# First layer's MLP: the last six pairs of hidden blocks by seven products, gated sums added to x by accumulating DMAs, squares on ScalarE

## The chip, the cores and the metric

One core of one Trainium2 chip runs the whole program. The metric is the device time of one execution in microseconds: 1545.13, 1548.43 and 1548.74 in three runs, median 1548.43. The profile's names for the engines are PE (TensorE's matmuls), PEld (its weight loads), DVE (VectorE), ACT (ScalarE), POOL (GpSimd) and SP (SyncE, which issues most of the DMAs).

## The reference

An inference step of a transformer with two layers over 640 tokens (512 latent, 128 context) of width 1024, with different weights in each layer. Each layer has a mixer and then an MLP with 4096 hidden columns; both read a normalised x that is shifted and scaled, and both add their output to x times a gate. Shift, scale and gate (six vectors of 1024 per layer, one set for latent and one for context tokens) come from a conditioning vector by a matrix product, the adaLN modulation. Cut to what matters:

```python
def squared_relu_mlp(h, w1, w2):
    return jnp.square(jax.nn.relu(h @ w1)) @ w2

def modulate(x, g, shift, scale):
    return rmsnorm(x, g) * (1 + scale) + shift

def trunk_layer(x, mod, p, mix_fn):
    shift1, scale1, gate1, shift2, scale2, gate2 = jnp.split(mod, N_MOD, axis=-1)
    y, ctx_state = mix_fn(modulate(x, p['norm1'], shift1, scale1))
    x = x + gate1 * y
    x = x + gate2 * squared_relu_mlp(modulate(x, p['norm2'], shift2, scale2), p['w1'], p['w2'])
    return x, ctx_state
```

## The kernel before

**Layout.** Features lie on the 128 partitions, tokens along the free dimension; x is one SBUF tile of 8 blocks of 128 features by 640 tokens. A product over all tokens is made in two halves of 384 and 256 tokens (HALVES). The context tokens have gates of their own, so the gated sum of a second half is two instructions of 128 columns (REGIONS).

**Precision.** Every operand is split in two fp32r parts, a rounded one and the remainder, and every product is three matmuls (mm3, lines 248 to 250). A weight unit of 128x1024 is loaded by SP into one of three raw buffers; ScalarE casts it (line 239), VectorE makes the difference (line 240); the result takes one of four `hl` buffers.

**The MLP.** The 4096 hidden columns go in eight groups of 512. A group has two pairs of hidden blocks, each pair 2 x 128 columns. The first product gives a pair's hidden values, which are squared after the relu and split; the second product multiplies a group's four hidden tiles with its rows of the second weight and adds the gated result to x, for eight blocks of output features (m) and two token halves. In program order the first product of group j+1 stands before the second product of group j.

A plain pair makes 96 matmuls of 384 or 256 columns, 320 on average; a group's second product makes 192. After a plain product ScalarE does the relu (line 1139) and the rounded square (line 1140), the full square is made by POOL in the first layer (line 1144) and by ScalarE in the second (line 1142), and VectorE takes the difference (line 1145).

**Seven products.** In the second layer, pairs 2 to 15 are made another way: each pair's product is seen as 2x2 blocks (two halves of the features by two hidden blocks; 320 tokens each) and made by seven products instead of eight, 84 matmuls of 320 columns. For this Blocks.sums makes sums and differences of blocks of the normalised activations once per layer, strip by strip (four strips), from an unsplit copy `hf` that ScalarE keeps (Blocks.keep); Pair.w2 makes four sums of weight blocks per pair (lines 1162 to 1172). Pair.rest puts the results together on VectorE and squares them at the end (Pair.square, lines 1195 to 1197). The first layer does all sixteen pairs plainly.

**Gated sums.** gate_add (line 428) reads the PSUM bank, multiplies by the gate and adds to x, on VectorE: one instruction for a first half, two for a second one.

**adaLN tiles.** ada_steps and ada_tile (lines 168 to 179) make 128 modulation values for both sets of tokens: a 512 KB load into one of the same three raw buffers and two instructions on VectorE (line 174). 80 of these stand in the first layer: 24 before its MLP, 56 in it. The first eight of the 56 give gate2, the gate of this very MLP; the other 48 are the second layer's. They stand in the program between the weight units of both products: eight in a group, twelve in the first.

**What sets the order.** The kernel writes its operations in program order; a planner of the framework, which has a time model of its own, orders each engine's list from it, with the program order as priority. Buffers come from pools: `a` (12 of 2x640), `b` (6 of the same), `p` (5 of 640: relu and square tiles `rr` and `rq`), `t2` (3 of 384), raw (3) and hl (4); PSUM has four single banks and two double ones.

Of the kernel before, what the change touches and what calls it, by code (L numbers as in the profile page):

```python
# [56 lines left out]
def step_kernel(ctx, tc, xT, wf, wt, wt3, wo1, wo2, wq, wkvs, wada, wnat, wnat2, vec, rows, fnorm, cvec, cache, kpec,  # L57
# [29 lines left out]
    def nm(s):  # L87
        uid[0] += 1
        return f"{s}_{uid[0]}"
# [30 lines left out]
    def f(ap):  # L120
        return ap.bitcast(F32)
# [269 lines left out]
    class Blocks(Modulate):  # L391
# [8 lines left out]
        def sums(self, s):  # L400
            if s == 0:
                self.op = {k: [None] * 4 for k in ("b11", "b21", "b22", "t1", "t2", "t3", "t4")}
            op = self.op
            if s % 2 == 0:
                t3 = phase["me"].tile([128, 2, 2, HT], F32R, tag="t3", bufs=1, name=nm("t3")) if s else \
                    tb([128, 2, 2, HT], "t3")
                for k, two in (("t2", ta([128, 2, 2, HT], "t2")), ("t3", t3), ("t1", ta([128, 2, 2, HT], "t1"))):
                    op[k][s], op[k][s + 1] = two[:, 0], two[:, 1]
            h1, h2 = self.h[s], self.h[4 + s]
            op["b11"][s], op["b21"][s], op["b22"][s] = h1[:, :, :HT], h2[:, :, :HT], h2[:, :, HT:]  # L410
            op["t4"][s] = h1[:, :, HT:]
            fx = self.hf[s]
            b11, b12, b21, b22 = fx[:, 0, :HT], fx[:, 0, HT:], fx[:, 1, :HT], fx[:, 1, HT:]
            t3, t2_ = tmp2([128, HT], "t3"), tmp2([128, HT], "t2")
            nc.vector.tensor_sub(t3, b12, b22)
            nc.vector.tensor_sub(b12, b11, b12)
            nc.vector.tensor_add(t2_, b22, b12)
            nc.vector.tensor_sub(b21, b21, t2_)
            for k, src in (("t2", t2_), ("t3", t3), ("t1", b12), ("t4", b21)):
                split(op[k][s][:, 0, :], op[k][s][:, 1, :], src)  # L420
# [15 lines left out]
    def layer(l, h, next_norm, nxt):  # L436
# [669 lines left out]
        mod.step(0, K_PAIRS[6])  # L1106
        mod.step(0, K_PAIRS[7])
        close_phase()
        if blocks:
            open_phase(f"mlp{l}", me=1)  # L1110

        me = phase.get("me")

        class Pair:

# [3 lines left out]

            def __init__(self, p, u=None):
                self.p = p
                pool = (lambda: me.tile([128, 2, TOK], F32R, tag="u", bufs=2, name=nm("u"))) if p % 3 == 0 \
                    else (lambda: tb([128, 2, TOK], "u"))
                self.u = u or [pool(), pool()]
                self.r, self.q = [None] * 2, [None] * 2

            def plain(self, us, i, half, tail=None):

                t0, n = HALVES[half]
                ps = bank("w1")
                u, ui = us[i], self.u[i]
                for z, k in enumerate(K_PAIRS):
                    mm3(ps[:, :n], (u[:, 0, 128 * k:128 * (k + 1)], u[:, 1, 128 * k:128 * (k + 1)]),
                        act(mod.h, k, t0, n), z == 0, z == KT - 1)
                r, q = tp([128, 384], "rr")[:, :n], tp([128, 384], "rq")[:, :n]
                hh = ui[:, 0, t0:t0 + n]
                nc.scalar.activation(r, ps[:, :n], AF.Relu)  # L1139
                nc.scalar.activation(hh, r, AF.Square)  # L1140
                if blocks:
                    nc.scalar.activation(q, r, AF.Square)
                else:
                    nc.gpsimd.tensor_mul(q, r, r)  # L1144
                nc.vector.tensor_sub(ui[:, 1, t0:t0 + n], q, f(hh))

            def load(self):
# [81 lines left out]
            return x_.u  # L1229

        def two_plain(j):
            get = ta if j % 2 == 0 else tb
            two = [Pair(2 * j + i, [get([128, 2, TOK], "u") for _ in range(2)]) for i in range(2)]
            for i in range(4):
                w = load_unit(wf[l, U_W1 + 4 * j + i])
                for half in range(2):
                    two[i // 2].plain([w, w], i % 2, half)
                if l == 0:
                    ada_steps(2 if j == 1 else 1)
            return two[0].u + two[1].u  # L1240

        def mlp2_tile(ut, u, m, half, nrm):
# [5 lines left out]
            gate_add(ps, m, half, l, 40, nrm)  # L1248

        def mlp2(j, ut):  # L1250
            if j < 7:
                for i in range(4):
                    u = load_unit(wf[l, U_W2 + 4 * j + i])
                    for m in (2 * i, 2 * i + 1):
                        for half in range(2):
                            mlp2_tile(ut, u, m, half, None)
                    if l == 0:
                        ada_steps(1)
            else:
                us = [load_unit(wf[l, U_W2 + 4 * j + i]) for i in range(4)]  # L1260
                for m in range(8):
                    mlp2_tile(ut, us[m // 2], m, 0, next_norm)
                for m in range(8):
                    mlp2_tile(ut, us[m // 2], m, 1, next_norm)
                    if m >= 2:
                        nxt.step(0, m - 2)
                for half, k in ((0, 6), (0, 7)) + tuple((1, k) for k in range(KT)):
                    nxt.step(half, k)

        head = [Pair(p, None if blocks else [ta([128, 2, TOK], "u") for _ in range(2)]) for p in range(2)]  # L1270
# [8 lines left out]
        if blocks:  # L1279
            for s in range(4):  # L1280
                mod.sums(s)
            mlp2(0, us)
            us = full(2) + full(3)
            for j in range(1, 8):
                if j < 7:
                    nxt_us = full(2 * j + 2)
                mlp2(j, us)
                if j < 7:
                    us = nxt_us + full(2 * j + 3)
            close_phase()  # L1290
            del phase["me"]
        else:
            for j in range(8):
                cur = us
                if j < 7:
                    us = two_plain(j + 1)
                mlp2(j, cur)


    open_phase("mix0", lay=1, pt=3)  # L1300
# [152 lines left out]
```

## Time and profile before

| | us |
|---|---|
| median of three runs | 1548.43 |
| profiled execution | 1544.02 |
| its span | 1542.1 |
| PE busy | 1473.7 (96%) |
| DVE busy | 1131.9 (73%) |
| ACT busy | 668.9 (43%) |
| POOL busy | 248.2 (16%) |
| the first layer's MLP | 342.6 to 805.5 |
| the second layer's MLP | 1089.8 to 1533 |

Times inside the span are counted from its start. Busy time is what an engine spent in instructions that the profile counts as work; register, semaphore and DMA-issuing instructions are not in it. PE's matmuls are pipelined, so a busy PE is not PE at its peak. The granted clock is the share of full speed that TensorE was allowed: 1.00 is 2.4 GHz. In a row of the timeline, the bracket says how long the engine had stood before the instruction and what released it.

### The profile page before, as it was taken

How to read it: one execution, taken by the hardware profiler on the slowest of the kernel's cores; microseconds unless marked ns; L12 is line 12 of the kernel's file. 1: busy time of each engine (PE TensorE's matmuls, PEld its weight loads, DVE VectorE, ACT ScalarE, POOL GpSimd, SP SyncE). 2: the span in 40 equal slices, each digit the busy share in tenths (PEclk: the TensorE clock that was granted, in tenths of full speed). 3: DMA queues.
4: the chain of work that ended last, by engine and by line, in shares of the span. 5: the costliest groups of instructions: out<-in, count | busy, mean ns of one | idle time of the engine just before them, and what ended most of it. 6: DMA issues, size and time to landing. Idle time of an engine off the chain costs nothing.

```text
span 1542.1 us, 25203 instructions
## 1 busy us (share of the span) xinstructions
PE 1473.7 (96%) x9716; PEld 1415.8 (92%) x9716; DVE 1131.9 (73%) x2210; ACT 668.9 (43%) x1400; POOL 248.2 (16%) x245
## 2 busy tenths in 40 slices
PE   6898999989999999999999999998999999999997
PEld 2698988979999999999999989898899999999996
DVE  5988878869978778876458666686886676566655
ACT  3544556745222322232236445675835244324422
POOL 2133103343211210120021110222300000000002
PEclk9899999999999999999999989999999999999999
DMA  8544321333555455444212311011222223123211
GB/s 312 199 136 139 100 66 45 103 94 111 190 164 164 139 151 162 151 142 146 66 48 64 123 43 37 30 49 45 83 69 96 69 83 96 57 81 96 83 55 69
DMA packets 50103, 160.22 MB, mean 104 GB/s; under 512 B 6208, under 2 KB 10304, under 8 KB 49984
## 3 DMA queue, kind: packets, MB, share of 16 engines
q1 hardware_dynamic: 48320, 154.68, 31.4%
q10 hardware_dynamic: 1664, 3.93, 0.7%
q8 instruction: 77, 1.26, 0.3%
q14 instruction: 42, 0.34, 0.1%
HBM read 155.55 MB, written 3.05 MB: 103 GB/s over the span
## 4 chain that ended last, share of the span: by engine, by line
PE 78%; DVE 11%; ACT 4%; issue 2%; POOL 1%; DMA 1%; POOLq 0%; DVEq 0%; ACTq 0%; SPq 0%
PE w L250 13%; PE w L249 13%; PE w L248 13%; PE qcd L248 2%; PE fm L248 2%; PE qcd L250 2%; PE fm L250 2%; PE qcd L249 2%; PE fm L249 2%; PE out L248 2%; PE tm L249 2%; PE tm L248 2%; PE tm L250 2%; PE out L249 2%; PE out L250 2%
## 5 line engine op out<-in xcount | busy, mean ns | idle before, releaser
L248 PE MATMUL w<-u,hl 128*128 128x384 f32 (+1 forms) x1024 | 316.9, 310 | 5.0 <-DVE x L428 2.7
L249 PE MATMUL w<-u,hl 128*128 128x384 f32 (+1 forms) x1024 | 317.0, 310 | 0.7 <-DVE u L1197 0.7
L250 PE MATMUL w<-u,hl 128*128 128x384 f32 (+1 forms) x1024 | 316.9, 310 | 0.4 <-DVE hl L240 0.4
L239 ACT CAST hl<-raw 128x1024 fp32r<-128x1024 f32 (+3 forms) x176 | 170.7, 973 | 267.3 <-PE w L250 155.8
L240 DVE TENSOR_TENSOR hl<-raw,hl 128x1024 fp32r<-128x1024 f32 (+3 forms) x156 | 182.7, 1174 | 36.8 <-ACT hl L239 36.4
L428 DVE SCALAR_TENSOR_TENSOR x<-w,mod,x 128x128 f32<-128x128 f32 (+1 forms) x384 | 154.4, 434 | 66.8 <-PE w L250 65.8
L248 PEld LDWEIGHTS w<-u,hl 128*128 128x128 f32 x1024 | 194.4, 190 | 5.8 <-DVE x L428 2.9
L249 PEld LDWEIGHTS w<-u,hl 128*128 128x128 f32 x1024 | 194.7, 190 | 1.0 <-DVE u L1197 1.0
L250 PEld LDWEIGHTS w<-u,hl 128*128 128x128 f32 x1024 | 194.6, 190 | 0.6 <-DVE hl L240 0.6
L249 PE MATMUL w<-h,hl 128*128 128x384 f32 (+1 forms) x576 | 178.4, 311 | 3.8 <-DVE h L369 3.8
L250 PE MATMUL w<-h,hl 128*128 128x384 f32 (+1 forms) x576 | 178.3, 310 | 0.0
L248 PE MATMUL w<-h,hl 128*128 128x384 f32 (+1 forms) x576 | 177.7, 310 | 0.0
L174 DVE CUSTOM_DVE_ANT_0 junk<-adaw,cb,vec 128x1024 f32<-128x1024 f32 x84 | 112.4, 1338 | 61.1 <-DMA adaw<-in_wada 61.1
L270 POOL TENSOR_TENSOR ss<-ss,sq 128x384 f32<-128x384 f32 (+1 forms) x40 | 37.3, 932 | 502.3 <-ACT sq L269 501.6
L1144 POOL TENSOR_TENSOR rq<-rr 128x384 f32<-128x384 f32 (+1 forms) x64 | 65.1, 1018 | 328.9 <-ACT rr L1139 273.3
L174 DVE CUSTOM_DVE_ANT_0 adaw<-adaw,cb,vec 128x1024 f32<-128x1024 f32 x84 | 116.0, 1381 | 1.3
L249 PEld LDWEIGHTS w<-h,hl 128*128 128x128 f32 x576 | 109.4, 190 | 5.7 <-DVE h L369 5.7
L248 PEld LDWEIGHTS w<-h,hl 128*128 128x128 f32 x576 | 109.6, 190 | 0.0
L250 PEld LDWEIGHTS w<-h,hl 128*128 128x128 f32 x576 | 109.6, 190 | 0.0
L248 PE MATMUL fm<-h,hl 128*128 128x256 f32 (+1 forms) x288 | 93.8, 326 | 2.1 <-DVE u L582 2.1
L249 PE MATMUL fm<-h,hl 128*128 128x256 f32 (+1 forms) x288 | 91.6, 318 | 0.0
L250 PE MATMUL fm<-h,hl 128*128 128x256 f32 (+1 forms) x288 | 91.4, 317 | 0.0
(329 smaller groups left out, 3399.6 us busy)
## 6 DMA issues: line engine op xcount, KB each, us to landing
raw<-in_wf SPq DMA_DIRECT2D x146, 512.0 KB, 3.5
adaw<-in_wada SPq DMA_DIRECT2D x84, 512.0 KB, 3.6
raw<-in_wo SPq DMA_DIRECT2D x24, 384.0 KB, 3.1
adan<-in_wnat SPq DMA_DIRECT2D x12, 512.0 KB, 8.3
raw<-in_wt SPq DMA_DIRECT2D x16, 384.0 KB, 3.2
x<-in_xT ACTq DMA_DIRECT2D x4, 640.0 KB, 7.2
raw<-in_wt SPq DMA_DIRECT2D x8, 288.0 KB, 2.8
raw<-in_wo SPq DMA_DIRECT2D x4, 512.0 KB, 3.7
```

What stands on the lines that cost most here:

```text
L174: nc.vector.tensor_tensor_reduce(out=raw if g else junk, in0=raw, in1=cb[:, g, :], op0=ALU.mult, op1=ALU.add, scale=1.0, scalar=vecs[l][:, ...
L239: nc.scalar.copy(hl[:, 0, :n], raw[:, :n])
L240: (nc.gpsimd if pool else nc.vector).tensor_sub(hl[:, 1, :n], raw[:, :n], f(hl[:, 0, :n]))
L248: nc.tensor.matmul(out, lhsT=lhs[0], rhs=rhs[0], start=start, stop=False, skip_group_check=more)
L249: nc.tensor.matmul(out, lhsT=lhs[0], rhs=rhs[1], start=False, stop=False, skip_group_check=more)
L250: nc.tensor.matmul(out, lhsT=lhs[1], rhs=rhs[0], start=False, stop=stop, skip_group_check=more)
L270: (nc.gpsimd if pool else nc.vector).tensor_add(self.s[:, t0:t0 + n], self.s[:, t0:t0 + n], sq[:, :n])
L428: nc.vector.scalar_tensor_tensor(out=x[:, m, t0:t0 + n], in0=ps[:, t0 - b0:t0 - b0 + n], scalar=mods[l][g][:, gate + m:gate + m + 1], in1= ...
L1144: nc.gpsimd.tensor_mul(q, r, r)
```

## The change

In the first layer's MLP, a number J0 = 5 divides the work (in the second layer it is 1, which is what that layer did before). Groups 0 to 4 are made plainly, groups 5 to 7 (pairs 10 to 15) by seven products. The order is then that of the second layer: two plain pairs, the sums of the activations' blocks, the second product of group 4, and pairs by seven products from there. The sums thus stand between the second product of group 3 and that of group 4. There is no kept `hf` in the first layer: sums rebuilds it with two VectorE additions of 640 columns per strip, into buffers of the pool `p`.

The gated sum of the first layer's groups 0 to 6 becomes ScalarE work: per block m, three evictions with the gate as scale into a `go` tile of 640 columns (also from the pool `p`), and one accumulating DMA from GpSimd's queue that adds the tile to x in SBUF. Group 7 keeps gate_add. The full square of a plain pair moves from POOL to ScalarE in the first layer too. The 56 adaLN tiles are dealt anew: 13 in the first group, 11 in each of the next three, then 4, 3 and 3. Finally the hidden tiles of plain groups take the pools `a` and `b` in swapped turns, and the pool `me` is opened in both layers.

```diff
+            if self.hf is None:
+                fx = [tp([128, TOK], "hf") for _ in range(2)]
+                for z, hz in enumerate((h1, h2)):
+                    nc.vector.tensor_add(fx[z], f(hz[:, 0, :]), f(hz[:, 1, :]))
+            else:
+                fx = [self.hf[s][:, z, :] for z in range(2)]
...
+        J0 = 1 if blocks else 5
...
-                if blocks:
-                    nc.scalar.activation(q, r, AF.Square)
-                else:
-                    nc.gpsimd.tensor_mul(q, r, r)
+                nc.scalar.activation(q, r, AF.Square)
...
-                if l == 0:
-                    ada_steps(2 if j == 1 else 1)
+                ada_steps((3, 2, 2, 1)[i] if j == 1 else (2, 2, 1, 1)[i])
...
+            if go is None:
+                gate_add(ps, m, half, l, 40, nrm)
+                return
+            for a, w, g in REGIONS[half]:
+                nc.scalar.activation(go[:, a:a + w], ps[:, a - t0:a - t0 + w], AF.Copy,
+                                     scale=mods[l][g][:, 40 + m:41 + m])
+            if half:
+                nc.gpsimd.dma_start(out=x[:, m, :], in_=go, accum_op=ALU.add)
...
+                        go = tp([128, TOK], "go") if l == 0 else None
...
-                        ada_steps(1)
+                        ada_steps((2, 1, 1, 1)[i] if j < J0 - 1 else (1, 1, 1, int(j < J0))[i])
...
+        for j in range(J0 - 1):
+            cur = us
+            us = two_plain(j + 1)
+            mlp2(j, cur)
+        for s in range(4):
+            mod.sums(s)
+        mlp2(J0 - 1, us)
+        us = full(2 * J0) + full(2 * J0 + 1)
+        for j in range(J0, 8):
+            if j < 7:
+                nxt_us = full(2 * j + 2)
+            mlp2(j, us)
+            if j < 7:
+                us = nxt_us + full(2 * j + 3)
```

## Rows read from the trace of the kernel before

**Rows 1.** Chain of waits on the page, whole span, by engine.

```profile
PE 78%; DVE 11%; ACT 4%; issue 2%; POOL 1%; DMA 1%; POOLq 0%; DVEq 0%; ACTq 0%; SPq 0%
```

**Rows 2.** Stretches: length, PE, PEld, DVE, ACT, POOL, granted clock, DMA share, GB/s.

```profile
377.56:405.69 28.13, 28.13 (x195) 28.13 (x193) 27.84 (x40) 9.72 (x18) 9.37 (x7) 1.00 0.63 207
...
438.33:494.57 56.24, 56.24 (x387) 56.24 (x385) 44.58 (x89) 14.82 (x24) 8.45 (x8) 1.00 0.52 161
...
1221.02:1274.20 53.18, 53.18 (x362) 52.77 (x361) 35.00 (x58) 20.62 (x28) 0.00 (x0) 1.00 0.25 80
```

**Rows 3.** Timeline of PE at period borders: start, length, line, tile.

```profile
438.33 0.34 PE L248 MATMUL w<-h,hl 128*128 128x384 f32 x1
...
494.57 0.34 PE L248 MATMUL w<-h,hl 128*128 128x384 f32 x1
...
1221.02 0.31 PE L248 MATMUL qa<-h,hl 128*128 128x320 f32 x1
1221.17 0.31 PE L249 MATMUL qa<-h,hl 128*128 128x320 f32 x1
...
1274.20 0.31 PE L248 MATMUL qa<-h,hl 128*128 128x320 f32 x1
```

**Rows 4.** Timeline from 412 to 416; its last row, a stretch.

```profile
412.60 0.28 PE L250 MATMUL w<-u,hl 128*128 128x256 f32 x1
415.60 0.45 PE L248 MATMUL w<-u,hl 128*128 128x384 f32 x1 [2.72 <-DVE x L428]
...
412.12 1.05 ACT L239 CAST hl<-raw 128x1024 fp32r<-128x1024 f32 x1 [3.38 <-DMA raw<-in_wf]
...
413.38 1.29 DVE L174 CUSTOM_DVE_ANT_0 junk<-adaw,cb,vec 128x1024 f32<-128x1024 f32 x1 [0.58 <-DMA adaw<-in_wada]
...
414.93 0.61 DVE L428 SCALAR_TENSOR_TENSOR x<-w,mod,x 128x384 f32<-128x384 f32 x1
...
415.40:418.50 3.10, 2.90 (x13) 2.91 (x14) 3.10 (x7) 1.05 (x1) 0.00 (x0) 0.76 0.34 90
```

**Rows 5.** Timeline of PE in the second layer's last product.

```profile
1503.44 0.34 PE L250 MATMUL w<-u,hl 128*128 128x384 f32 x1
1504.53 0.96 PE L248 MATMUL w<-u,hl 128*128 128x384 f32 x4 [0.75 <-ACT u L1195]
...
1506.16 0.44 PE L249 MATMUL w<-u,hl 128*128 128x384 f32 x1 [0.67 <-DVE u L1197]
```

**Rows 6.** VectorE by line and form, 438.33 to 775.77: busy, mean ns | idle.

```profile
L240 DVE TENSOR_TENSOR hl<-raw,hl 128x1024 fp32r<-128x1024 f32 x48 | 59.1, 1231 | 11.4 <-ACT hl L239 11.2
L174 DVE CUSTOM_DVE_ANT_0 adaw<-adaw,cb,vec 128x1024 f32<-128x1024 f32 x41 | 56.3, 1374 | 0.5
L174 DVE CUSTOM_DVE_ANT_0 junk<-adaw,cb,vec 128x1024 f32<-128x1024 f32 x41 | 53.5, 1304 | 56.5 <-DMA adaw<-in_wada 56.5
```

**Rows 7.** VectorE by line and form, 1108 to 1131.

```profile
L254 DVE TENSOR_TENSOR t<-t,t 128x320 fp32r<-128x320 f32 x8 | 3.8, 486 | 0.0
```

**Rows 8.** Groups of VectorE by line, whole span.

```profile
L428 DVE SCALAR_TENSOR_TENSOR x<-w,mod,x 128x128 f32<-128x128 f32 (+1 forms) x384 | 154.4, 434 | 66.8 <-PE w L250 65.8
...
L1197 DVE TENSOR_TENSOR u<-rr,u 128x640 fp32r<-128x640 f32 x28 | 23.0, 821 | 1.4 <-ACT rr L1196 1.3
```

**Rows 9.** Single lines: shortest, mean, longest ns, when first and last.

```profile
L848 ACT ACTIVATE cqT<-cqt,vec x8: 462/527/582, 226.7 to 978.4; 128x384 fp32r<-128x384 f32 x4, 128x256 fp32r<-128x256 f32 x4
...
L633 ACT ACTIVATE xc<-fm x6: 272/274/299, 128.8 to 896.8; 128x128 f32<-128x128 f32 x6
...
L1142 ACT ACTIVATE rq<-rr x8: 411/465/520, 1103.8 to 1125.0; 128x384 f32<-128x384 f32 x4, 128x256 f32<-128x256 f32 x4
...
L1144 POOL TENSOR_TENSOR rq<-rr x64: 609/828/1914, 357.6 to 748.4; 128x384 f32<-128x384 f32 x32, 128x256 f32<-128x256 f32 x32
```

**Rows 10.** DMA issues: tile, queue, count, size, us to landing.

```profile
adaw<-in_wada SPq DMA_DIRECT2D x84, 512.0 KB, 3.6
...
rq<-in_rope_q SPq DMA_DIRECT2D x2, 320.0 KB, 5.3
```

More of the change, by code (lines that the diff above doesn't have):

```diff
@@ L411, in sums @@
             op["t4"][s] = h1[:, :, HT:]
-            fx = self.hf[s]
-            b11, b12, b21, b22 = fx[:, 0, :HT], fx[:, 0, HT:], fx[:, 1, :HT], fx[:, 1, HT:]
+            if self.hf is None:
[4 more added lines that the diff above has]
+                fx = [self.hf[s][:, z, :] for z in range(2)]
+            b11, b12, b21, b22 = fx[0][:, :HT], fx[0][:, HT:], fx[1][:, :HT], fx[1][:, HT:]
             t3, t2_ = tmp2([128, HT], "t3"), tmp2([128, HT], "t2")
@@ L1108, in layer @@
         close_phase()
-        if blocks:
-            open_phase(f"mlp{l}", me=1)
-        me = phase.get("me")
+        open_phase(f"mlp{l}", me=1)
+        me = phase["me"]
+        J0 = 1 if blocks else 5
         class Pair:
@@ L1123, in __init__ @@
                 self.p = p
-                pool = (lambda: me.tile([128, 2, TOK], F32R, tag="u", bufs=2, name=nm("u"))) if p % 3 == 0 \
+                pool = (lambda: me.tile([128, 2, TOK], F32R, tag="u", bufs=2, name=nm("u"))) if (p - J0 + 1) % 3 == 0 \
                     else (lambda: tb([128, 2, TOK], "u"))
@@ L1140, in plain @@
                 nc.scalar.activation(hh, r, AF.Square)
-                if blocks:
-                    nc.scalar.activation(q, r, AF.Square)
-                else:
-                    nc.gpsimd.tensor_mul(q, r, r)
+                nc.scalar.activation(q, r, AF.Square)
                 nc.vector.tensor_sub(ui[:, 1, t0:t0 + n], q, f(hh))
@@ L1231, in two_plain @@
         def two_plain(j):
-            get = ta if j % 2 == 0 else tb
+            get = tb if j % 2 == 0 else ta
             two = [Pair(2 * j + i, [get([128, 2, TOK], "u") for _ in range(2)]) for i in range(2)]
@@ L1237, in two_plain, with mlp2_tile @@
                     two[i // 2].plain([w, w], i % 2, half)
-                if l == 0:
-                    ada_steps(2 if j == 1 else 1)
+                ada_steps((3, 2, 2, 1)[i] if j == 1 else (2, 2, 1, 1)[i])
             return two[0].u + two[1].u
-        def mlp2_tile(ut, u, m, half, nrm):
+        def mlp2_tile(ut, u, m, half, nrm, go=None):
             t0, n = HALVES[half]
@@ L1247, in mlp2_tile @@
                 mm3(ps[:, :n], (u[:, 0, c0:c0 + 128], u[:, 1, c0:c0 + 128]), act(ut, k, t0, n), k == 0, k == 3)
-            gate_add(ps, m, half, l, 40, nrm)
+            if go is None:
[6 more added lines that the diff above has]
+                nc.gpsimd.dma_start(out=x[:, m, :], in_=go, accum_op=ALU.add)
         def mlp2(j, ut):
@@ L1254, in mlp2 @@
                     for m in (2 * i, 2 * i + 1):
+                        go = tp([128, TOK], "go") if l == 0 else None
                         for half in range(2):
-                            mlp2_tile(ut, u, m, half, None)
+                            mlp2_tile(ut, u, m, half, None, go)
                     if l == 0:
-                        ada_steps(1)
+                        ada_steps((2, 1, 1, 1)[i] if j < J0 - 1 else (1, 1, 1, int(j < J0))[i])
             else:
@@ L1268, in mlp2 @@
                     nxt.step(half, k)
-        head = [Pair(p, None if blocks else [ta([128, 2, TOK], "u") for _ in range(2)]) for p in range(2)]
+        head = [Pair(p, None if blocks else [tb([128, 2, TOK], "u") for _ in range(2)]) for p in range(2)]
         ws = [load_unit(wf[l, U_W1 + i], pool=True) for i in range(4)]
@@ L1278, in layer @@
         us = head[0].u + head[1].u
[L1279 to L1297, printed above, removed]
+        for j in range(J0 - 1):
[12 more added lines that the diff above has]
+                us = nxt_us + full(2 * j + 3)
+        close_phase()
+        del phase["me"]
     open_phase("mix0", lay=1, pt=3)
```

## The prediction

> **What bounds the kernel now.** I read the page's chain of waits first: TensorE carries 78% of it [rows 1]. Then the table of stretches. In the first layer's MLP one group of 512 hidden columns (two plain pairs, then their second product) takes 56.24 us, in which PE is busy 56.24 us at a granted clock of 1.00; in the second layer one group by seven products takes 53.18 us, also without a hole [rows 2]. The timeline of PE gives the borders of these periods [rows 3]. So in both MLPs the number of matmul columns sets the time, and everything else counts only where it opens a hole in PE. The waits show one such hole in the first layer's MLP, in the first second product [rows 4], and the tail of the second layer shows what a last pair by seven products leaves open [rows 5]. The reader should see there who released PE: VectorE, behind a DMA.
>
> The sum is made against the profiled execution, 1544.02 us (span 1542.1 and 1.9 around it). The median of the runs is 1548.43, 4.4 above it; I apply the difference to the median. A difference under 0.3% (4.65 us) can't be told from no change with this kernel.
>
> **1. Fewer matmuls: -9.2 us.** Groups 5, 6 and 7 of the first layer change from plain to seven products: 2 x 84 matmuls of 320 columns in place of 2 x 96 of 320 on average. The second layer does exactly this with the same code, so the price is the difference of periods: 56.24 - 53.18 = 3.06 us a group, 9.2 for three, on PE, which is the path [rows 2, 3].
>
> **2. A tail before the last second product: +2.1 us.** In group 7 the last pair is followed at once by the product that needs its squares. In the second layer PE stands there from 1503.44 to 1504.53 and again from about 1505.2 to 1506.16, released by the squares and the difference (L1195, L1197), where 0.17 a matmul is usual [rows 5]: about 2 us. Today the first layer has no such place. Ends: 0.5 (if other PE work is moved in) and 4 (with casts of the next layer ahead of the squares on ScalarE).
>
> **3. The hole in group 0: -3.6 us.** From 405.69 to 438.33 the second product takes 32.64 us where half a group is 28.12 [rows 2, 3]: 4.5 lost. PE stands from 412.60 to 415.60; before L428 there is an adaLN tile on VectorE that waited for its DMA until 413.38, and L428 itself comes at 414.93 [rows 4]. L428 leaves VectorE here: the gated sum goes to ScalarE, which waits for no adaLN tile. VectorE also loses 24 x 0.434 = 10.4 us in this product [rows 8], while one adaLN tile (2.7 us [rows 6]) is added, and POOL's squares go, which take 0.83 us alone and up to 1.91 beside VectorE [rows 9]. What can be late next is ScalarE: at 412.12 it had just stood 3.38 us in a cast, waiting for a weight load [rows 4], and a gated sum behind such a cast waits too. So I take 3.6 of the 4.5; ends -4.5 and 0.
>
> **4. The block sums: +4.0 us.** Here the change adds work in a place of its own, between groups 3 and 4. Per strip VectorE makes two copies of 640 columns, four sums of 320 and four differences of 320: 2 x 0.82 + 8 x 0.49 = 5.6 us by durations [rows 7, 8], four strips 22 us, some 19 with the overlap of neighbours. ScalarE adds 16 casts off the path. The strips' results go into buffers that group 3's squares hold until its second product ends, at a time T. VectorE's list from T until PE needs the first sum (28.1 + 1.8 = 29.9 us later): sums 19, two adaLN tiles 5.4 (two of four are done ahead), three casts' differences at 1.23 [rows 6] and four weight sums, some 31 in all. That alone is a hole of about 1 us. A nearer limit is the tag of five buffers from which the strips' copies (two each) and the new gate tiles both come: in program order all eight copies stand ahead of group 4's first gate tile. If buffers are handed out in that order, that tile is free once the second strip is done, about T + 8.5; PE has four banks, 2 x 3.51 = 7.0 us. That gives a hole of 2 to 3 us. A hole costs more than its length: after the 2.8 us of 412.60 the granted clock is 0.76 over the next 3 us [rows 4], and the loss was 4.5. So 2.5 x 4.5 / 2.8 = 4.0. Ends: 0 (sums done in VectorE's idle time) and 10.
> The Trainium skill, "TensorE: Matmul & The Clock Gate", Part 1, says that an idle PE falls to half its clock and has to earn it back. The trace agrees: 0.76 behind the hole is a mix of the two levels, 1.2 and 2.4 GHz. By the hole alone this step would be 2.5 and the sum 1.5 lower.
>
> **5. More adaLN tiles per group: +0.8 us.** Groups 1 to 3 take 11 tiles where 8 were; the total stays. VectorE's 44.6 us a group [rows 2] become 44.6 - 10.4 + 3 x 2.7 = 42.3. But each tile also waits 56.5 / 41 = 1.4 us for its load [rows 6], since tiles and weight units share three raw buffers in one queue order, and SP takes 19 loads a group, not 16. 42.3 + 11 x 1.4 = 57.7 against 56.2: 1.5 us late a group, 4.5 in three. The four split-weight buffers let units run up to three units (21 us) ahead, which covers it, if the lead has been rebuilt after group 0. Ends 0 and 4.5.
>
> **6. Gated sums by ScalarE and DMA, squares on ScalarE: +0.5 us.** ScalarE is busy 14.8 us a group [rows 2]. Added: 16 squares' halves by one square each, 8 x 0.47 = 3.7 us, and eight times one 384-column and two 128-column evictions with a scale: between 0.58 + 2 x 0.27 = 1.1 and 0.58 + 2 x 0.46 = 1.5 us [rows 9], 9 to 12 us. Some 30 of 56 us: it stays beside PE. POOL loses eight squares and issues eight DMAs. An accumulating DMA of 327 KB isn't in this trace; the nearest landings are 3.6 us (512 KB) and 5.3 us (320 KB) [rows 10]. Its tile is then held for some 6 to 8 us from the first write, two of five buffers at one tile every 3.51 us: free. Its cover is those five buffers; the price without it is rival C. Later readers of x (the last second product) come 12 us of matmuls after the last DMA. Ends -1 and +5.
> The next layer's first loads now wait for the space of the closed MLP pool until the last pair is done; the 28 us of the last product cover that.
>
> **Sum:** -9.2 + 2.1 - 3.6 + 4.0 + 0.8 + 0.5 = -5.4 us: 1538.6 for the profiled execution, 1543.0 against the median.
>
> **Rivals.**
> A, no hole at the sums: VectorE's idle time ahead of T takes the copies, or buffers are handed to whoever is ready first. For it: VectorE is idle 11.7 us a group [rows 2]. Against it: before T the results have no place. -9.2 + 2.1 - 4.5 + 0.5 + 0.5 = -10.6: 1537.8.
> B, the gain goes back into holes: the one in group 0 stays, because ScalarE stands in casts, and the sums cost 5. For it: ScalarE stood 3.38 us at that very place [rows 4]. -9.2 + 2.1 + 0 + 5 + 1.5 = -0.6: 1547.8, no change.
> C, slower: the tag of five buffers. If two strips' copies are made while group 3's second product still needs gate tiles, four of five buffers are held until T, and each pair of halves waits for one buffer: 3.5 filling, 1.1 on ScalarE, 3.6 or more until landing, some 8.5 us where 3.51 is usual, 5 us each. From two such tiles on the gain is gone; with four it is -9.2 + 2.1 - 3.6 + 20 + 1.3 = +10.6: 1559.0. For it: the copies need nothing but h, which is ready long before. Against it: in program order they come behind. The Trainium skill, "DMA: Bandwidth & Descriptors", section "SWDGE vs HWDGE vs iDMA", adds that a DMA issued by GpSimd has its descriptors written by GpSimd into SBUF, which VectorE can hold up; no DMA from POOL is in this trace, and only POOL's own products show such slowing (0.83 to 1.91 us) [rows 9]. A longer landing brings C nearer.
>
> **Chances.** The forecast 0.50, A 0.18, B 0.20, C 0.12. The forecast's own range is -8 to -2.5 us; some three tenths of it lie within 0.3%. So faster by over 0.3%: 0.35 + 0.18 = 0.53; within 0.3%: 0.15 + 0.20 = 0.35; slower: 0.12. The range 1535.5 to 1551.5 holds the forecast, nearly all of A and B, and the mild end of C.
>
> **What would show it.** Step 1: the last groups of the first layer at 53.2 us a period with 320-column matmuls, dense. Step 2: two holes of about 1 us in the last product, released by L1195 and L1197's successors. Step 3: group 0's second product at 28 to 29 us. Step 4: between groups 3 and 5 a hole released by ScalarE (a gated sum, a late gate tile) or by a strip's difference, and a clock under 1.00 behind it. Step 5: groups 1 to 3 at 56.2. Step 6: DMA landings of gate tiles under 6 us. The prediction is wrong if a group's period by seven products isn't 53.2 in the first layer, if any hole is longer than 10 us, or if ScalarE's evictions hold PE in the plain groups.

## The result, and the profile after

The changed kernel is slower: median 1570.88 us (1570.31 to 1573.33) against 1547.42 (four runs of each kernel), ratio 1.0173 (1.0147 to 1.0200). The forecast was 1543.0 with a range to 1551.5.

The page's chain of waits of the changed kernel comes first, shares by engine and then by line:

```profile
PE 50%; DVE 11%; DMA 9%; ACT 3%; issue 3%; POOL 0%; POOLq 0%; DVEq 0%; ACTq 0%; SPq 0%
DMA adaw<-in_wada 8%; PE w L250 7%; PE w L249 7%; PE w L248 7%; DVE junk L174 3%; PE qcd L248 3%; PE qcd L250 3%; PE qcd L249 3%; PE qa L248 1%; PE qa L250 1%; PE qa L249 1%; DVE hl L240 1%; PE fm L248 1%; DVE adaw L174 1%; PE fm L250 1%
```

PE carried 78% of it before [rows 1]; now the loads of adaLN tiles alone carry 8% and VectorE's products on them (L174) 4%. Stretches of the changed kernel (columns as in rows 2): groups 1, 2 and 3, then the second product of group 4, then a group by seven products:

```profile
441.61:502.58 60.97, 56.40 (x386) 56.20 (x384) 40.99 (x74) 25.50 (x54) 6.09 (x7) 0.99 0.78 215
502.58:565.53 62.95, 59.33 (x384) 59.12 (x384) 40.82 (x61) 26.48 (x57) 6.96 (x8) 0.95 0.72 199
565.53:623.44 57.91, 57.91 (x384) 57.91 (x385) 37.07 (x68) 27.29 (x59) 7.82 (x9) 0.97 0.72 190
623.44:668.31 44.87, 30.55 (x195) 30.14 (x193) 34.98 (x61) 19.33 (x44) 6.97 (x9) 0.85 0.58 138
734.19:787.81 53.62, 53.51 (x362) 52.89 (x361) 30.69 (x42) 28.95 (x52) 6.96 (x8) 1.00 0.63 157
```

A plain group took 56.24 with a DMA share of 0.52 [rows 2]. Now it takes 57.9 to 63.0 at 0.72 to 0.78, though VectorE has less to do (37 to 41 against 44.6) and POOL only issues the DMAs (6 to 8). The second product of group 4 takes 44.87 where 28.1 is usual. The seven products keep their period but for 0.4 (53.2 before). The prediction named three signs of being wrong; two of them are here, a hole over 10 us and ScalarE's evictions holding PE in the plain groups.

**Where the time went.** The first layer's MLP runs from 345.22 to 832.23, 487.0 us against 463.0. (2.7 us of the spans' difference of 27.3 had come up before the MLP began, in work that the change doesn't touch; those are left aside.) Counting PE's time from one matmul's start to the next above the usual pace (0.1735 us for 384 columns, 0.1467 for 320, 0.119 for 256) gives the losses. "Sums" is the second product of group 4 (in f4, of group 3) and, where it lost too, the pair behind it. MLP and losses are of the one profiled run of each kernel, the ratio is of all its runs: the profile of e4 is the slowest of its six (1559.79, median 1553.65), those of e7, e9d, e10 and f4 are the fastest of theirs (e7: 1540.64, median 1545.94).

| kernel | ratio to before (95%) | MLP | groups 0-3 | sums | later |
|---|---|---|---|---|---|
| before | 1 | 463.0 | 4.5 | - | 0.4 |
| the change | 1.0173 (1.0147-1.0200) | 487.0 | 18.3 | 16.8 | 3.1 |
| e1 deal of before | 1.0040 (1.0021-1.0058) | 469.2 | 0 | 14.6 | 5.7 |
| e2 no DMAs | 1.0041 (1.0022-1.0060) | 467.5 | 3.2 | 11.4 | 3.5 |
| e3 gated sums on VectorE | 1.0022 (1.0008-1.0035) | 463.0 | 6.9 | 3.0 | 4.1 |
| e4 new deal alone | 1.0057 (1.0031-1.0084) | 473.8 | 15.2 | - | 0.4 |
| e5 gate path alone | 0.9961 (0.9946-0.9976) | 459.4 | 0.9 | - | 0.4 |
| e12 seven products alone | 1.0043 (1.0024-1.0063) | 473.2 | 1.1 | 14.0 | 9.7 |
| e7 own buffers | 1.0015 (0.9999-1.0030) | 461.6 | 4.3 | 5.5 | 2.9 |
| e9a copies apart | 1.0123 (1.0091-1.0154) | 479.9 | 24.9 | 1.2 | 4.4 |
| e9b e7 and e9a | 0.9980 (0.9962-0.9999) | 459.6 | 6.3 | 0 | 4.2 |
| e9d e7, e9a and e1 | 0.9999 (0.9980-1.0018) | 458.1 | 2.2 | 0 | 6.5 |
| e10 e3 and e7 | 0.9935 (0.9911-0.9959) | 451.6 | 0 | 0 | 2.6 |
| e11 e10 and e9a | 1.0009 (0.9991-1.0026) | 465.8 | 7.0 | 7.0 | 2.6 |
| f1 gate tiles apart | 1.0091 (1.0072-1.0109) | 479.9 | 21.8 | 4.7 | 4.3 |
| f2 half of each DMA | 1.0080 (1.0053-1.0107) | 476.9 | 9.8 | 15.3 | 2.6 |
| f4 e10 with J0 = 4 | 0.9940 (0.9919-0.9961) | 449.4 | 0 | 0.9 | 2.4 |

Each kernel loses 6.1 to 6.8 more in the first 35 us, as before. Without losses the MLP would be 452.0 us before and 442.7 in the change: the 9.2 us of fewer matmuls are there, under 44 us of holes.

**A hole in the plain groups.** Timeline of the changed kernel at the end of group 1 (SPq is SP's queue of DMA issues):

```profile
494.60 0.33 SPq L237 DMA_DIRECT2D raw<-in_wf  x1
495.70 1.22 DVE L240 TENSOR_TENSOR hl<-raw,hl 128x1024 fp32r<-128x1024 f32 x1
...
501.00 1.04 ACT L239 CAST hl<-raw 128x1024 fp32r<-128x1024 f32 x1 [8.90 <-DMA raw<-in_wf]
501.95 1.56 ACT L1253 ACTIVATE go<-w,mod 128x384 f32<-128x384 f32 x4
...
502.58 0.69 PE L248 MATMUL w<-h,hl 128*128 128x384 f32 x1 [4.57 <-ACT go L1253]
```

Read it backwards. PE waits for a bank that a gated sum (L1253) empties; the gated sum stands on ScalarE's list behind a cast that has waited 8.90 us for its weight load; that load was issued at 494.60, when VectorE had finished an adaLN tile and so freed a raw buffer, and it took up to 6.4 us. After the hole PE runs its next 24 matmuls in 7.09 us, 4.17 at full pace, at a granted clock of 0.56:

```profile
502.58:509.67 7.09, 7.09 (x24) 7.09 (x25) 3.48 (x5) 2.38 (x6) 1.74 (x2) 0.56 0.71 155
```

What the DMA engines did from 488 to 503 (their busy tenths in 40 slices, then the queues: packets, MB, share of 16 engines; q0 is the accumulating DMAs):

```profile
DMA  9999999999499799999999998996786987997420
...
q1 hardware_dynamic: 750, 2.68, 52.8%
q0 software_dynamic: 432, 0.98, 38.0%
```

The engines are busy nearly all of the time, and 38% of their time goes to 0.98 MB of gate tiles. From the page, over the whole span:

```profile
q1 hardware_dynamic: 48320, 154.68, 30.5%
q0 software_dynamic: 8064, 18.35, 6.7%
...
x<-go POOLq DMA_DIRECT2D x56, 320.0 KB, 5.5
```

6.7% of 1569.4 us over 56 DMAs is 1.88 us of all sixteen engines for one gate tile, against 1.6 for a load of 512 KB (30.5% x 1569.4 x 0.524 / 154.68). All eight of a group fall into its second product: 15 of 28.1 us.

**The hole at the sums.** Timeline of the changed kernel:

```profile
631.74 1.29 DVE L174 CUSTOM_DVE_ANT_0 junk<-adaw,cb,vec 128x1024 f32<-128x1024 f32 x1 [2.37 <-DMA adaw<-in_wada]
...
634.33 2.29 DVE L415 TENSOR_TENSOR hf<-h 128x640 f32<-128x640 f32 x3
...
643.31 0.48 DVE L254 TENSOR_TENSOR h<-hf,h 128x320 fp32r<-128x320 f32 x1
...
643.93 0.57 ACT L1253 ACTIVATE go<-w,mod 128x384 f32<-128x384 f32 x1
...
644.56 0.69 PE L248 MATMUL w<-u,hl 128*128 128x384 f32 x1 [13.93 <-ACT go L1253]
```

Group 3 ends at 623.44, but VectorE first does adaLN tiles that wait for their loads and comes to the first copy (L415) 10.9 us later. Two strips take until 643.79; then the first gate tile of group 4 gets its buffer. So the hole has two parts: the late start, and two strips that stand between a gate tile and the pool of five.

That copies wait for the pool is seen where no gate tile takes it (e3, e10, e12, f1, f4): there the first copy comes some 22 to 25 us before the product ahead of the sums ends, in e10 at 581.53 (end 606.1), in f1 at 606.10 (end 627.8):

```profile
581.53 0.81 DVE L415 TENSOR_TENSOR hf<-h 128x640 f32<-128x640 f32 x1
...
606.10 2.29 DVE L415 TENSOR_TENSOR hf<-h 128x640 f32<-128x640 f32 x3
```

**The tail**, in the last second product, answering to rows 5:

```profile
805.53 0.97 PE L248 MATMUL w<-u,hl 128*128 128x384 f32 x4 [0.92 <-ACT u L1197]
...
807.16 0.45 PE L249 MATMUL w<-u,hl 128*128 128x384 f32 x1 [0.66 <-DVE u L1199]
```

### The profile page after: what moved, and what is told of

It is laid out like the page before. It is cut to its first block, busy times and chain, and to the rows that moved or that the text cites. A ratio compares the mean times of both kernels' runs of the same rounds, so it can differ in the third digit from the quotient of the medians.

```text
span 1569.4 us, 25185 instructions
## 1 busy us (share of the span) xinstructions
PE 1473.5 (94%) x9644; PEld 1411.8 (90%) x9644; DVE 1116.4 (71%) x2136; ACT 766.6 (49%) x1636; POOL 232.2 (15%) x237
## 3 DMA queue, kind: packets, MB, share of 16 engines
q1 hardware_dynamic: 48320, 154.68, 30.5%
q0 software_dynamic: 8064, 18.35, 6.7%
## 4 chain that ended last, share of the span: by engine, by line
PE 50%; DVE 11%; DMA 9%; ACT 3%; issue 3%; POOL 0%; POOLq 0%; DVEq 0%; ACTq 0%; SPq 0%
DMA adaw<-in_wada 8%; PE w L250 7%; PE w L249 7%; PE w L248 7%; DVE junk L174 3%; PE qcd L248 3%; PE qcd L250 3%; PE qcd L249 3%; PE qa L248 1%; PE qa L250 1%; PE qa L249 1%; DVE hl L240 1%; PE fm L248 1%; DVE adaw L174 1%; PE fm L250 1%
## 5 line engine op out<-in xcount | busy, mean ns | idle before, releaser
L239 ACT CAST hl<-raw 128x1024 fp32r<-128x1024 f32 (+3 forms) x164 | 158.2, 968 | 190.2 <-DMA raw<-in_wf 90.4
L240 DVE TENSOR_TENSOR hl<-raw,hl 128x1024 fp32r<-128x1024 f32 (+3 forms) x144 | 166.7, 1160 | 33.8 <-ACT hl L239 33.4
L174 DVE CUSTOM_DVE_ANT_0 junk<-adaw,cb,vec 128x1024 f32<-128x1024 f32 x84 | 109.6, 1306 | 74.3 <-DMA adaw<-in_wada 74.3
L248 PE MATMUL w<-h,hl 128*128 128x384 f32 (+1 forms) x384 | 121.2, 317 | 8.2 <-ACT go L1253 8.2
L249 PE MATMUL w<-h,hl 128*128 128x384 f32 (+1 forms) x384 | 120.9, 317 | 4.5 <-DVE h L369 4.5
L433 DVE SCALAR_TENSOR_TENSOR x<-w,mod,x 128x128 f32<-128x128 f32 (+1 forms) x216 | 87.4, 435 | 51.7 <-PE w L250 50.9
L250 PE MATMUL w<-h,hl 128*128 128x384 f32 (+1 forms) x384 | 120.9, 315 | 0.0
L174 DVE CUSTOM_DVE_ANT_0 adaw<-adaw,cb,vec 128x1024 f32<-128x1024 f32 x84 | 111.3, 1326 | 1.9
L1256 POOL DMA_DIRECT2D x<-go x56 | 49.0, 876 | 383.1 <-ACT go L1253 318.9
L253 ACT CAST hl<-s 128x1024 fp32r<-128x1024 f32 x40 | 41.9, 1047 | 123.9 <-PE w L250 83.7
L1253 ACT ACTIVATE go<-w,mod 128x384 f32<-128x384 f32 x168 | 64.4, 437 | 45.7 <-PE w L250 36.8
L248 PEld LDWEIGHTS w<-h,hl 128*128 128x128 f32 x384 | 75.0, 195 | 8.6 <-ACT go L1253 8.6
```

The lines of the kernel that those rows point to most:

```text
L174: nc.vector.tensor_tensor_reduce(out=raw if g else junk, in0=raw, in1=cb[:, g, :], op0=ALU.mult, op1=ALU.add, scale=1.0, scalar=vecs[l][:, ...
L239: nc.scalar.copy(hl[:, 0, :n], raw[:, :n])
L240: (nc.gpsimd if pool else nc.vector).tensor_sub(hl[:, 1, :n], raw[:, :n], f(hl[:, 0, :n]))
L248: nc.tensor.matmul(out, lhsT=lhs[0], rhs=rhs[0], start=start, stop=False, skip_group_check=more)
L249: nc.tensor.matmul(out, lhsT=lhs[0], rhs=rhs[1], start=False, stop=False, skip_group_check=more)
L250: nc.tensor.matmul(out, lhsT=lhs[1], rhs=rhs[0], start=False, stop=stop, skip_group_check=more)
```

## Experiments: the ring and the traffic

Three theories stood at first: the ring of three raw buffers (R), the accumulating DMAs' traffic (T), the order on ScalarE (S). The ring takes the loads of weight units and of adaLN tiles in SP's order; a group is called dense when PE has no hole in it.

**e1, the deal of before.**

```diff
-                ada_steps((3, 2, 2, 1)[i] if j == 1 else (2, 2, 1, 1)[i])
+                ada_steps(2 if j == 1 else 1)
...
-                        ada_steps((2, 1, 1, 1)[i] if j < J0 - 1 else (1, 1, 1, int(j < J0))[i])
+                        ada_steps(1 if j < J0 - 1 else 2)
```

> The changed kernel with the adaLN tiles of the first layer's MLP dealt as before in the plain groups (12, then 8 a group) and the rest behind them (8, 8, 4 in groups 4 to 6). Theory R (the ring): weight units and adaLN tiles share three raw buffers in one order, a buffer comes free only when VectorE is done with it, and 19 loads at some 3.3 us don't fit into the 56.24 us of a plain group; that costs the 13.1 us of groups 1 to 3 and makes VectorE 11 us late at the block sums. R expects 56.2 us a group for groups 1 to 3, a loss of 4 to 6 us in the second product of group 4 in place of 16.75, and 1544 to 1552 us. Theory T (traffic): the accumulating DMAs lengthen the loads, so with 16 loads about half of the loss stays: 1555 to 1560. Theory S (ScalarE's order): gated sums stand behind casts and behind the strips' casts on ScalarE, whatever the number of tiles: 1565 to 1571.

Groups 0 to 3 lose nothing, as R said, group 0 included. Group 1:

```profile
438.06:494.31 56.25, 56.25 (x387) 56.25 (x386) 36.76 (x63) 26.68 (x56) 6.96 (x8) 1.00 0.75 203
```

The DMA share is as high as in the change, 0.75, and PE has no hole: the traffic does no harm to 16 loads. But the sums still lose 14.6, which R had put at 4 to 6. The timeline there:

```profile
614.65 1.04 ACT L239 CAST hl<-raw 128x1024 fp32r<-128x1024 f32 x1 [7.04 <-DMA raw<-in_wf]
...
615.30 2.30 DVE L415 TENSOR_TENSOR hf<-h 128x640 f32<-128x640 f32 x3
...
624.85 0.58 ACT L1253 ACTIVATE go<-w,mod 128x384 f32<-128x384 f32 x1 [0.80 <-DVE h L254]
```

The gate tile is released by the second strip's last difference. VectorE began the copies 8.5 us after group 3's end (606.8), behind two adaLN tiles, for the first of which it had stood 3.9 us.

**e2, no accumulating DMAs.**

```diff
-            if half:
-                nc.gpsimd.dma_start(out=x[:, m, :], in_=go, accum_op=ALU.add)
```

> The changed kernel without the 56 accumulating DMAs; ScalarE still writes the gate tiles. The products of groups 0 to 6 are left out of x. R expects that 11 tiles a group are too many all the same: groups 1 to 3 lose 9 to 13 us, the sums 12 to 17, time 1562 to 1571. T expects groups 1 to 3 at 56.2 us, adaLN loads at 3.5 us throughout, and 1545 to 1550. S expects 1563 to 1571.

```profile
437.14:493.67 56.53, 56.40 (x387) 56.20 (x385) 40.60 (x74) 25.82 (x54) 0.00 (x0) 1.00 0.55 178
```

Group 1 is nearly dense with all 11 tiles: R's number fails here, and T holds for it and for the time; group 2 still loses 2.9 and the sums 11.4. So neither is enough alone for the loss of the change: 19 loads a group get through with 3.2 lost without the traffic, the traffic is harmless with 16 loads, and together they lose 18.3 us. S, for which neither mattered, falls: the order on ScalarE only passes the delay on to PE.

**e4, the new deal alone, on the kernel before.**

```diff
-                if l == 0:
-                    ada_steps(2 if j == 1 else 1)
+                if l == 0 and j < 5:
+                    ada_steps((3, 2, 2, 1)[i] if j == 1 else (2, 2, 1, 1)[i])
...
-                        ada_steps(1)
+                        ada_steps((2, 1, 1, 1)[i] if j < 4 else (1, 1, 1, int(j < 5))[i])
```

> The kernel before with one edit: its adaLN tiles dealt 13, 11, 11, 11, 4, 3, 3 as in the change. Gated sums stay on VectorE, no accumulating DMA, no seven products. R expects groups 1 to 3 to lose 9 to 15 us in all (their periods 59 to 61 us) and 1556 to 1563. T and S expect no change, 1545 to 1550, since there is neither traffic nor a gated sum on ScalarE.

```profile
501.41:562.55 61.14, 56.78 (x386) 56.38 (x385) 50.90 (x85) 15.06 (x24) 7.89 (x8) 1.00 0.51 165
```

10.7 us more lost in groups 0 to 3, with no accumulating DMA (share 0.51); 8.9 of the losses are in groups 1 to 3, just under R's 9 to 15. The time, 1553.65, is below R's band and above that of T and S, which expected no loss. Here VectorE, on whose list the gated sums stand too, is what the ring waits for: busy 50.9 us against 44.6.

**e7, buffers of their own for the adaLN tiles** of groups 0 to 4:

```diff
+        def own(shape, s, dt):
+            return me.tile([128, 2, 512], F32, tag="s", bufs=2, name=nm(s)).rearrange("p a b -> p (a b)")
...
+                ada_steps((3, 2, 2, 1)[i] if j == 1 else (2, 2, 1, 1)[i], own)
...
-                        ada_steps((2, 1, 1, 1)[i] if j < J0 - 1 else (1, 1, 1, int(j < J0))[i])
+                        ada_steps((2, 1, 1, 1)[i] if j < J0 - 1 else (1, 1, 1, int(j < J0))[i], own if j < J0 else None)
```

> The changed kernel with one edit: the adaLN tiles of groups 0 to 4 are loaded into two buffers of their own (those that the weight sums use from group 5 on), so the ring of three holds weight units alone; the deal of 13, 11, 11, 11 stays. R expects groups 1 to 3 at 56.2 to 57 us, the second product of group 4 to lose 3 to 6 us, and 1544 to 1552. T expects loads still lengthened, half of the loss: 1555 to 1560. S expects 1563 to 1571.

```profile
436.50:492.74 56.24, 56.24 (x386) 56.24 (x385) 48.26 (x87) 26.84 (x56) 6.96 (x8) 1.00 0.84 246
```

All 11 tiles and all the traffic, a DMA share of 0.84, and a dense group. The engines could carry it; three buffers shared in one order could not keep enough loads on the way. A loss of 4.3 in group 2 (the expectation of e9b calls it group 3) and 5.5 at the sums stay. The edit gives more buffers and parts the two streams at once; five buffers shared by both were not run.

## Experiments: the tag, and traffic or hold

The tag is the pool `p` of five buffers, from which the strips' copies, the gate tiles and the squares come.

**e9a, the strips' copies apart.**

```diff
-                fx = [tp([128, TOK], "hf") for _ in range(2)]
+                fu = phase["me"].tile([128, 2, TOK], F32, tag="u", bufs=2, name=nm("hf"))
+                fx = [fu[:, z, :] for z in range(2)]
```

> The changed kernel with one edit: the unsplit copies of the strips are written into the two buffers for hidden tiles of the pool me (not in use before pair 10) instead of the five-buffer pool that the gate tiles use. The deal of 11 and the ring of three stay. Theory P (tag): the hole of 13.9 us in the second product of group 4 is a gate tile's wait for the buffers of the first two strips; P expects that hole at 0 to 4 us and 1557 to 1562 us on the scale of the changed kernel's 1570.9. Theory L (late VectorE): VectorE comes to the sums 11 us late, behind adaLN tiles whose loads are late, and weight units' differences stand behind the sums; L expects 9 us or more still lost there and 1565 to 1571.

The sums lose 1.2 in place of 16.8: theory P, and L falls as the cause, though late VectorE sets how long the hole of P is. The edit does more than it says: the first four copies find their buffers free and are made over 200 us earlier. The groups lose 24.9, 6.6 more than in the change, and why is open. By the ratio, 1.0123, the time on the changed kernel's scale is some 1566: above P's band, which had no such loss in the groups, and in L's.

**e9b and e9d**, e9a's edit with e7's, then with e1's deal as well.

> Both edits: the strips' copies in the pool me's hidden tiles, and adaLN tiles of groups 0 to 4 in two buffers of their own; deal of 11. Against the one with own buffers alone (ratio 1.0015 to the kernel before, 5.4 us lost at the sums, 4.3 in group 3): P expects the 5.4 to go to 0 to 1 and a ratio of 0.998 to 0.999; L expects it to stay, ratio 1.001 to 1.002.

> Those two edits and the deal of before (12, 8, 8, 8, then 8, 8, 4). All three theories of the ring expect groups 0 to 3 at 56.2 us with no hole (group 0 too, 4.5 us better than in the kernel before); P expects a loss of 0 to 2 us at the sums. The gain from the 252 fewer matmul groups then shows: 1544.8 - 4.5 - 6.5 + 1 = 1535, ratio 0.992 to 0.995. If the moved tiles open holes in groups 5 and 6 (one of 2.9 us was there with the deal alone), 0.995 to 0.998.

e9b: as P said, nothing is lost at the sums, and the version is just faster than before. e9d misses both its bands: its groups are dense but for 2.2, and its MLP is 4.9 us shorter than before in the profiled run (1539.69), but the median is 1545.02 and the ratio 0.9999; where the other runs lose it is not known. (The 252 in its expectation is wrong: the pages have 9644 matmuls against 9716, 72 fewer.)

**f1, the gate tiles apart**, and **f2, half of each DMA**:

```diff
+                    gu = me.tile([128, 2, TOK], F32, tag="u", bufs=2, name=nm("go")) if l == 0 and j < J0 else None
...
-                        go = tp([128, TOK], "go") if l == 0 else None
+                        go = (gu[:, m % 2, :] if j < J0 else tp([128, TOK], "go")) if l == 0 else None
```

```diff
-                nc.gpsimd.dma_start(out=x[:, m, :], in_=go, accum_op=ALU.add)
+                nc.gpsimd.dma_start(out=x[:, m, :HT], in_=go[:, :HT], accum_op=ALU.add)
```

> The changed kernel with one edit: the gate tiles of groups 0 to 4 lie in the two buffers for hidden tiles of the pool me, two of them in each, and no longer in the five-buffer pool, which then serves only squares and the strips' copies. DMAs, deal of 11 and ring of three stay. If gate tiles, held until their DMA has landed, starve that pool (theory H, hold), the losses of groups 0 to 3 (18.3 us with the edge of group 4) and of the sums (16.8) both go: 0 to 5 us left, ratio 0.998 to 1.001. If the DMAs' time on the DMA engines makes the loads late (theory T with the ring), groups 0 to 3 still lose 13 to 25 us and only the sums gain (0 to 3 lost, as with the strips' copies apart): ratio 1.006 to 1.013.

> The changed kernel with accumulating DMAs of half the columns (320 of 640): the other half of the sums of groups 0 to 6 is left out of x. By the queue table 56 DMAs took 6.7% of 16 engines over the span, 1.88 us of all engines each, against 1.6 for a load of 512 KB; eight of them and ten loads make 31 us in a second product of 28.1. T expects half of the DMA time, 27 us, to fit: groups 0 to 3 lose 2 to 8 us in place of 18.3, ratio 1.004 to 1.010 with the sums' hole of 11 to 15 left. H expects the hold to shrink only from some 5.5 us to 4: groups 0 to 3 lose 11 to 16, ratio 1.012 to 1.016.

f1: no gate tile holds the pool of five, and groups 0 to 3 still lose 21.8 (4.7 at the sums, more than T's 3): it is traffic, not hold. ScalarE again stood before casts for weight loads, 8.03 us ahead of the gated sum that ends group 1's hole. f2: 9.8 lost, between the two bands for the groups, the ratio in T's; with the whole DMA 18.3, with none 3.2, so the loss goes with the bytes. Group 1 of f2, its DMA share halfway between e2's and the change's:

```profile
435.15:494.86 59.71, 56.76 (x384) 56.36 (x384) 41.43 (x74) 26.15 (x57) 6.96 (x8) 1.00 0.67 191
```

## Experiments: each part alone, and a faster version

**e5, the gate path alone** (gated sums by ScalarE and accumulating DMAs, and the squares on ScalarE, added to the kernel before), and **e3**, the change without it:

```diff
-                        go = tp([128, TOK], "go") if l == 0 else None
+                        go = None
```

> The kernel before with one part of the change alone: gated sums of groups 0 to 6 by ScalarE and accumulating DMAs, squares on ScalarE. All pairs plain, adaLN deal of before. If the gate path does harm only together with 19 loads a group, groups 1 to 6 stay at 56.2 us and group 0 gains some 4 us as it did with the deal of before in the changed kernel: ratio 0.996 to 0.999. If the path harms by itself (its traffic, or gate tiles behind casts on ScalarE), groups 1 to 6 lose 2 to 5 us each: ratio 1.006 to 1.015.

> The changed kernel with the gated sums of the first layer back on VectorE (no gate tiles, no accumulating DMAs); deal of 11, ring of three, squares on ScalarE and seven products stay. R expects the losses of the deal alone in groups 0 to 3 (about 11 us more than in the kernel before) and, since VectorE has 10.4 us a group more to do and the gated sums stand behind 22 us of block sums, 10 to 16 us at the sums: ratio 1.006 to 1.014. T expects no loss in groups 1 to 3 without the traffic: ratio 0.999 to 1.004.

e5 is faster than before: the hole of group 0 falls from 4.5 to 0.4, and groups 1 to 6 stay dense but for 0.5, at a DMA share of 0.74. So the path is a gain where 16 loads a group stand. e3 without it is 24 us shorter in the MLP than the change. The ratio is T's; the 6.9 us that groups 2 and 3 still lose, where T expected none, are R's kind of loss, smaller than its 11. Its group 0 is dense with 13 tiles and the gated sums on VectorE.

**e12, seven products alone** (e3's and e1's edits):

> Seven products for pairs 10 to 15 without the gate path and without the new deal: gated sums on VectorE, adaLN tiles 12, 8, 8, 8, then 8, 8, 4; squares on ScalarE. By the steps of the prediction: fewer matmuls -9.2, tail +2.1, the hole of group 0 stays (4.5 as before), the sums +3 (as with the gated sums on VectorE and the deal of 11): -4, ratio 0.997. If VectorE, with gated sums and two tiles a unit in groups 4 to 6, falls behind there: +3 to +8, ratio 0.999 to 1.003.

Slower, beyond both forecasts. From the sums to the next pairs VectorE is the bound (the stretch, then PE's waits from 380 to 900: us in total, times, longest):

```profile
607.51:681.70 74.19, 65.71 (x411) 62.61 (x409) 65.56 (x123) 26.33 (x40) 0.00 (x0) 0.95 0.38 121
```

```profile
PE w L250 <- DVE hl L240: 4.8, 4, 1.8
PE qa L250 <- DVE hl L254: 4.2, 2, 2.3
```

Two tiles a unit there, gated sums and 22 us of sums are too much for VectorE. The deal of the change leaves one tile a unit there; e3, which differs from e12 by that deal alone, loses 3.0 at the sums in place of 14.0.

**e10, e3's and e7's edits; e11, with e9a's too; f4, e10 with J0 = 4** (and the pools `a` and `b` in the turns of before).

> The changed kernel with gated sums on VectorE and, for the adaLN tiles of groups 0 to 4, two buffers of their own; deal of 11. With the gate path gone (20.1 us of losses left in that MLP, 6.9 of them in groups 2 and 3) the ring theory expects the 6.9 to go, and the sums at 3 or less: MLP at 453 to 457 us against 463, ratio 0.993 to 0.997. If those 6.9 us come from VectorE's load alone (busy in all of a group's time), they stay: ratio 1.000 to 1.003.

> The last one with the strips' copies in the pool me's hidden tiles too. No gate tile competes for the five-buffer tag now, so theory P expects little here: the sums lose 0 to 2 us less than in the last one, ratio 0.993 to 0.997. Late VectorE (the sums stand ahead of gated sums and weight units' differences on its list, 22 us) would keep the loss at 3 us or more.

> The version with gated sums on VectorE and own buffers for adaLN tiles (ratio 0.9935), with group 4 by seven products as well (J0 = 4; adaLN tiles 13, 11, 11, then 6, 5, 5, 5). Ring theory: own buffers cover groups 0 to 3, and VectorE has 35 + 5 x 2.7 = 48.5 of 53 us to do in a group by seven products: no hole, 3.1 us less, ratio 0.991 to 0.993. If the ring of three (used again from group 4 on) is too short there, holes of 2 to 4 us in each of groups 4 to 6: ratio 0.995 to 0.999.

e10 beats both kernels: 0.9935 (0.9911 to 0.9959). A plain group and one by seven products:

```profile
437.35:493.59 56.24, 56.24 (x386) 56.24 (x385) 52.49 (x105) 17.71 (x32) 0.00 (x0) 1.00 0.63 194
666.41:719.67 53.26, 53.26 (x363) 52.84 (x361) 41.60 (x71) 20.61 (x28) 0.00 (x0) 1.00 0.34 109
```

VectorE is busy 52.5 of 56.2 us, a larger share than in any of the plain groups above that lost, and PE has no hole: not VectorE's load but its waits for loads made it late there. e11 missed: PE waits 10.0 us for gated sums in groups 2 to 4, though only the copies' buffers differ from e10. Its last four copies come 2.0 to 4.6 us after group 3's product, where e10 has made all eight before its end; that fits the late VectorE of its expectation at the sums, and why groups 2 and 3 lose 7.0 as well stays open. f4's MLP is 2.2 us shorter than e10's (3.1 forecast), its ratio lies between its two bands, and the times can't tell it from e10.

## Why the prediction was wrong, step by step

1. Fewer matmuls, -9.2: right (452.0 to 442.7 without losses).
2. Tail, +2.1: right. The last group loses 2.6 against 0.4, by the two holes named.
3. Group 0, -3.6: measured +0.6 (5.1 lost against 4.5). The step holds by itself: e1 and e5 have 0 and 0.4 there. What was late next was ScalarE behind a cast, as named (it had stood 7.56 us for a weight load), with the loads of 13 tiles and the traffic behind it.
4. **The sums, +4.0: this step failed, by 12.8.** Measured 16.8. The place was right, the tag of five buffers with a gate tile behind the second strip (e9a: 1.2), and two strips took 9.4 us against 8.5 (half of the step's own 19 is 9.5). The failed part is the start: the step let the copies begin at T, the end of group 3; they began 10.9 us later, behind adaLN tiles that waited for loads (e1: 8.5). Its reason for T fails too: before T the results were to have no place, but with the gate tiles out of that pool, by one edit in f1, all eight copies and six of the sixteen results are made before T (in e10 as well). That is the mechanism of rival A; in the change the gate tiles keep it out.
5. **More tiles a group, +0.8: this step failed, by 12.4, with step 6.** Measured 13.2 in groups 1 to 3. It took each tile's wait for its load at the 1.4 us of before [rows 6] and let a lead of three units cover the rest. The same change put 56 more DMAs on the engines, and the wait is no constant: 2.0 us a tile in groups 1 to 3 of the change, 1.5 in e2 without the DMAs (VectorE by line, last figure over the count):

```profile
L174 DVE CUSTOM_DVE_ANT_0 junk<-adaw,cb,vec 128x1024 f32<-128x1024 f32 x31 | 40.1, 1293 | 61.8 <-DMA adaw<-in_wada 61.8
...
L174 DVE CUSTOM_DVE_ANT_0 junk<-adaw,cb,vec 128x1024 f32<-128x1024 f32 x32 | 41.4, 1292 | 49.1 <-DMA adaw<-in_wada 49.1
```

The step's own sum, busy time plus 11 waits, then gives 39.6 + 11 x 2.0 = 61.6 us a group, where 60.6 was measured. The lead covered about 1 us of it. Without the DMAs (e2) groups 1 to 3 lose 3.2, within the step's ends of 0 to 4.5: it is the two steps together that failed.

6. Gated sums by DMA, +0.5. It priced an accumulating DMA by its landing alone (3.6 to 5.3 us taken, 5.5 measured) and by the buffer that it holds, which f1 shows to cost nothing in the plain groups. It left out the DMA engines' time: 1.88 us a tile. ScalarE's load, 25.5 to 27.3 us a group, was a little under the forecast's 30 (the middle figures of rows 9, from which that was worked out, are medians, not means). By themselves steps 3 and 6 were right: e5's MLP is 3.6 us shorter than before (3.1 by their sum).

The share of rows 2 could have warned: 0.52 on average, and another 15 us in each second product of 28.1. The sizes measured for the steps add up to -9.2 + 2.2 + 0.6 + 16.8 + 13.2 = 23.6 for the MLP, of 24.0.

Of the rivals, A and B are out. C named the five buffers and was nearest (1559.0), but its condition, copies made while group 3 still needs gate tiles, did not come about, and it had no term for the loads; that its time is the nearest is luck. The Trainium skill's rule cited there, on descriptors that GpSimd writes, was not put to a test of its own. The landing measured 5.5 us, where C had 3.6 or more; GpSimd's instruction that issues such a DMA took 0.87 us in the median and 1.07 at most, so no long hold-up shows there.

The Trainium skill has a rule that bears on step 6, "Collectives: The Full Stack", Part 3, "The bandwidth ceiling: the fold count and why AG ≠ RS ≠ AR": a DMA that adds reads two sources, and so puts twice the read traffic on its engines for each byte that it delivers (1.93 measured there, between cores). The trace agrees in size: per MB the accumulating queue took 6.7 / 18.35 = 0.365% against 30.5 / 154.68 = 0.197%, 1.85 times as much; that the second read is the reason no run here shows by itself.

## What to carry over

Price a DMA twice: by its landing, and by its time on the engines that the loads share, in the stretch where it falls. When two edits lean on one resource (here more loads in a ring of three buffers, and longer loads), test them together, since each alone can be harmless or a gain. If a ring is shared by two streams whose buffers are freed by an engine working in order, give the second stream its own buffers: that removed most of the stalls here without less work anywhere (e7: 18.3 to 4.3). Whether two more buffers shared by both would do as well is not tested. And ask of each pool who else takes from it: here the gate tiles kept the strips' copies from VectorE's free time.

## What the hardware showed

An accumulating DMA of 320 KB within SBUF took 1.88 us of sixteen DMA engines and 3.6 to 9.2 us to land; half of it 1.03 (3.7% of 1556.0 us over 56). Sixteen engines at 0.88 in a second product (e1, 466 to 494) still fed a dense PE. PE's idle time cost more than its length: after a hole of 4.57 us the granted clock was 0.56, a mix of the two levels 1.2 and 2.4 GHz, over the next 7.09, and the cost was 7.7; the sums, with a hole of 13.9, cost 16.8, at 0.85 over the stretch of 44.87.
